# Two feed-forward networks with seven block products in place of eight, in a one-core decoder layer

## The chip, the core and the metric

The kernel runs on one core of a Trainium2 chip. The core has five engines that run side by side, each in the order of its own queue: TensorE (PE in the profile; its weight loads have a row of their own, PEld), VectorE (DVE), ScalarE (ACT), GpSimd (POOL) and SyncE (SP), which here only issues DMA transfers. TensorE writes its sums to PSUM, eight banks of 128 partitions x 512 floats; the other operands lie in SBUF, 128 partitions wide, and device memory is reached by DMA. An engine waits for another on a semaphore.

The metric is the device time of one execution in microseconds. Lower is better.

## The reference

One layer of a hybrid decoder, for 1024 prompt tokens and 8 decoding sequences of one token, 1032 tokens together, with 1024 features each:

```python
def swiglu_half(x, g, w_gate, w_up, w_down):
    u = rmsnorm(x, g)
    return x + 0.5 * ((jax.nn.silu(u @ w_gate) * (u @ w_up)) @ w_down)

def hybrid_layer(...):
    h = swiglu_half(x, ffn1_norm, ...)          # 1024 -> 2816 -> 1024
    u = rmsnorm(h, mix_norm); z = u @ w_in      # latent attention, retention, two gates
    ...
    h = h + merged @ w_out
    h = swiglu_half(h, ffn2_norm, ...)
    gate = sigmoid(rmsnorm(h, ple_norm) @ w_ple_gate)
    return h + gate * (p_emb @ w_ple_proj)      # and a last rmsnorm
```

The change touches the two `swiglu_half` calls and what lies directly ahead of and behind them. Each is three products: 1032 x 1024 by 1024 x 2816 (gate and up) and 1032 x 2816 by 2816 x 1024 (down).

## The kernel before

Activations lie with the features on the partitions: a tile of 128 features by tokens. The tokens are cut into three chunks of 344 (`CHUNKS`). Every large product works on float32 values that are split in two: a high part in the format that TensorE takes at full rate (fp32r), made by a cast on ScalarE (L93), and the rest, made by a subtraction on VectorE (L94). `mm3` (L127 to L130) then multiplies high by high, high by low and low by high into one PSUM bank: three matmuls where plain arithmetic has one. A weight tile, 128 outputs by 1024 inputs, comes through `Ring.load` (L101): a DMA on SyncE's queue, then the split.

An FFN (`ffn`, L221) runs over the 22 blocks of 128 hidden features in groups of three (the last has four). For each block and chunk it makes the gate product and the up product, eight blocks of the inner dimension each (L230, L232), multiplies both by the reciprocal root `r` of the norm, applies Silu, multiplies, and splits the result into `mid` (L235 to L241). At the end of a group the down product adds its part to the residual `h` in SBUF (L274).

The norm is spread out. `norm_steps` (L183) multiplies the residual by the gain and splits it (L199 on ScalarE, L200 on VectorE), sums the squares (L148, then L149 on GpSimd), and `rstd` (L162) adds over the partitions with small matmuls (L169), takes the reciprocal root by three Newton steps on VectorE, and spreads it with matmuls (L177). The factor `r` is applied after the products, so that these need not wait for it. The steps of the next stage's norm are run one at a time between the products of the last group: `next(steps)` at L276 and in `wout` (ahead of FFN 2), with what remains kept in `pend` and drawn by `tick`. The residual stays in SBUF through an FFN; after FFN 1 a copy goes to device memory (`hs_d`, L331, on GpSimd's queue) and is read back at the merge (L1002).

After FFN 1 come the value tiles of the retention (`value_tile`, L314), 128 tokens by 256 columns over eight blocks of the inner dimension, whose evacuation needs `RT`, the factor `r` with tokens on partitions. After FFN 2 come the gate products of the per-layer embedding (`ple_gate`, L1034), over columns 0 to 400, 400 to 776 and 776 to 1032.

The order on each engine isn't that of the text. A planner takes the text's order as priority and fills an engine's free time with later instructions that it reckons to be ready; so in the first microseconds ScalarE works on `u` (L199) ahead of the weight cast (L93) that stands before it in the text. PSUM banks are taken in turn: 0 to 3 for products (`bank`), 4 to 7 for the norm and the retention (`cbank`).

## Time and profile before

| what | value |
|---|---|
| time of three runs, median (lowest to highest) | 2559.01 us (2556.11 to 2561.74) |
| profiled execution, its span | 2553.2 us (the page gives no other time of it; 5.8 us below the median of the runs) |
| TensorE busy | 2519.5 us, 99%, 16612 matmuls |
| VectorE, ScalarE, GpSimd busy | 49%, 26%, 8% |
| FFN 1, first FFN matmul to last | 7.6 to 778.8 us |
| FFN 2, first FFN matmul to last | 1665.6 to 2418.6 us |
| mean granted clock of TensorE | 0.996 of full speed |
| DMA | 171.08 MB, 67 GB/s on average |

The span runs from the first instruction to the last; what lies around it (the start and the end of the program) is not in the profile. Busy time of TensorE counts a matmul from its start to its modelled end, and these overlap, so the number to read is the pitch from one start to the next. In a group's row the parts are: source line, engine, operation, outputs and inputs with their shapes, the count, then busy microseconds and the mean nanoseconds of one, then the idle time ahead of it and what ended it. A row of a time stretch gives its length, then busy time and count for TensorE, its weight loads, VectorE, ScalarE and GpSimd, then the granted clock, the DMA share and GB/s. A row in order of time begins with start and duration in microseconds.

### The profile page before, as it was taken

To read this page: it belongs to the slowest core of one execution; us is meant where nothing else is said; L and a number is where in the kernel's file an instruction comes from. 1 tells how busy PE (TensorE), PEld (TensorE's weight loads), DVE (VectorE), ACT (ScalarE), POOL (GpSimd) and SP (SyncE) were. 2 spreads that over 40 slices of the span, in tenths; PEclk is the share of its full clock that TensorE was granted. 3 is DMA by queue.
4 is the path that set the end of the run, shared out by engine and by line. 5 is a ranking of instruction groups with operands and counts; after the bars stand their busy time and mean duration, and the time that the engine had idled before them with its cause. 6 is when DMAs were issued, how large, how long until landed. Compare 5 with 4: busy or idle time off the path is not lost.

```text
span 2553.2 us, 40552 instructions
## 1 busy us (share of the span) xinstructions
PE 2519.5 (99%) x16612; PEld 2433.6 (95%) x16612; DVE 1251.2 (49%) x2744; ACT 655.8 (26%) x1302; POOL 209.6 (8%) x247
## 2 busy tenths in 40 slices
...
GB/s 151 42 59 51 41 59 42 50 42 34 58 71 117 62 77 58 98 77 64 54 78 129 121 107 217 51 58 42 50 42 44 53 53 34 58 42 50 40 36 67
DMA packets 82507, 171.08 MB, mean 67 GB/s; under 512 B 9401, under 2 KB 51586, under 8 KB 82322
## 3 DMA queue, kind: packets, MB, share of 16 engines
...
q8 instruction: 130, 2.13, 0.3%
q14 instruction: 55, 0.45, 0.1%
...
## 4 chain that ended last, share of the span: by engine, by line
PE 94%; DVE 3%; DMA 1%; ACT 1%; issue 1%; POOL 0%; SPq 0%; POOLq 0%; DVEq 0%; ACTq 0%
PE ps L128 27%; PE ps L129 27%; PE ps L130 27%; PE ps L732 2%; PE ps L768 1%; PE ps L757 1%; PE ps L177 1%; PE ps L323 1%; PE ps L321 1%; PE ps L322 1%; DVE u L200 1%; PE ps L169 1%; DMA raw<-in_wout_dram 0%; PE ps L906 0%; PE ps L880 0%
## 5 line engine op out<-in xcount | busy, mean ns | idle before, releaser
L128 PE MATMUL ps<-u,w 128*128 128x344 f32 (+2 forms) x3072 | 990.6, 323 | 7.6 <-ACT w L93 7.6
L129 PE MATMUL ps<-u,w 128*128 128x344 f32 (+2 forms) x3072 | 987.0, 321 | 3.5 <-DVE u L200 3.5
L130 PE MATMUL ps<-u,w 128*128 128x344 f32 (+2 forms) x3072 | 982.8, 320 | 0.1
L128 PEld LDWEIGHTS ps<-u,w 128*128 128x128 f32 x3072 | 578.4, 188 | 9.6 <-ACT w L93 7.6
L129 PEld LDWEIGHTS ps<-u,w 128*128 128x128 f32 x3072 | 577.2, 188 | 6.4 <-DVE u L200 5.5
L130 PEld LDWEIGHTS ps<-u,w 128*128 128x128 f32 x3072 | 577.9, 188 | 1.1 <-DVE w L94 0.5
L93 ACT CAST w<-raw 128x1024 fp32r<-128x1024 f32 (+1 forms) x198 | 203.4, 1042 | 776.7 <-PE ps L130 757.0
L130 PE MATMUL ps<-mid,w 128*128 128x344 f32 x1248 | 399.7, 320 | 0.1
L129 PE MATMUL ps<-mid,w 128*128 128x344 f32 x1248 | 399.7, 320 | 0.0
L128 PE MATMUL ps<-mid,w 128*128 128x344 f32 x1248 | 399.6, 320 | 0.0
L274 DVE SCALAR_TENSOR_TENSOR h<-ps,h 128x344 f32<-128x344 f32 x336 | 172.0, 515 | 242.0 <-PE ps L130 239.8
L94 DVE TENSOR_TENSOR w<-raw,w 128x1024 fp32r<-128x1024 f32 (+1 forms) x198 | 239.1, 1219 | 63.5 <-ACT w L93 63.0
L130 PEld LDWEIGHTS ps<-mid,w 128*128 128x128 f32 x1248 | 235.4, 189 | 0.4 <-DVE w L94 0.4
L128 PEld LDWEIGHTS ps<-mid,w 128*128 128x128 f32 x1248 | 235.2, 188 | 0.0
L129 PEld LDWEIGHTS ps<-mid,w 128*128 128x128 f32 x1248 | 235.0, 188 | 0.0
L238 DVE TENSOR_TENSOR m<-ps,r 128x344 f32<-128x344 f32 x132 | 68.1, 516 | 336.4 <-PE ps L130 336.4
L149 POOL TENSOR_TENSOR acc<-acc,sq 128x344 f32<-128x344 f32 x83 | 84.1, 1013 | 1677.9 <-ACT sq L148 1676.6
L93 ACT CAST mid<-m 128x344 fp32r<-128x344 f32 x156 | 74.9, 480 | 353.3 <-DVE m L239 316.6
L235 DVE TENSOR_TENSOR sg<-ps,r 128x344 f32<-128x344 f32 x132 | 68.0, 515 | 167.5 <-PE ps L130 166.0
L236 ACT ACTIVATE sg<-sg 128x344 f32<-128x344 f32 x132 | 64.6, 489 | 227.8 <-DVE sg L235 227.8
L94 DVE TENSOR_TENSOR mid<-m,mid 128x344 fp32r<-128x344 f32 x156 | 80.9, 519 | 48.0 <-ACT mid L93 46.9
L200 DVE SCALAR_TENSOR_TENSOR u<-h,gains,u 128x344 fp32r<-128x344 f32 x96 | 65.1, 686 | 30.7 <-ACT u L199 30.6
(247 smaller groups left out, 2321.4 us busy)
## 6 DMA issues: line engine op xcount, KB each, us to landing
ct<-in_cache_dram SPq DMA_DIRECT2D x128, 128.0 KB, 2.1
...
hs_d<-h POOLq DMA_DIRECT2D x3, 1376.0 KB, 6.1
```

The source lines that it names most:

```text
L93: act.copy(dst_hi, src)
L94: dve.tensor_tensor(dst_lo, src, dst_hi.bitcast(F32), op=ALU.subtract)
L128: pe.matmul(ps, w[:, 0, ws], x[:, 0, xs], start=start, stop=False)
L129: pe.matmul(ps, w[:, 0, ws], x[:, 1, xs], start=False, stop=False)
L130: pe.matmul(ps, w[:, 1, ws], x[:, 0, xs], start=False, stop=stop)
L149: pool.tensor_tensor(acc, acc, sq[:, :n], op=ALU.add)
L200: dve.scalar_tensor_tensor(u[k][:, 1, xs], h[k][:, xs], gain(gi, k), u[k][:, 0, xs].bitcast(F32), op0=ALU.mult, op1=ALU.subtract)
L235: dve.tensor_tensor(s[:, :n], pg[:, :n], r[:, xs], op=ALU.mult)
L236: act.activation(s[:, :n], s[:, :n], AF.Silu)
L238: dve.tensor_tensor(m[:, :n], pu[:, :n], r[:, xs], op=ALU.mult)
L274: dve.scalar_tensor_tensor(hv, ps[:, :n], 0.5, hv, op0=ALU.mult, op1=ALU.add)
L732: pe.matmul(ps[:, :w], qc[hd][:, i * P:(i + 1) * P], kc[hd][:, j:j + w], start=True, stop=not diag)
```

## The change

Both FFNs compute each product as a two by two block product with seven multiplications in place of eight (the Winograd form of Strassen's method). The output tiles are taken in pairs, the inner dimension is halved, and the tokens are cut into two halves (`TPS`) of two quarters of 258 (`HC`). The multiplications need sums and differences of the blocks on both sides, and the results need sums.

- On the weight side `Stream` loads four 128 x 512 pieces (four DMAs on SyncE's queue), makes four sums on GpSimd and splits seven operands. `take` keeps five operands ahead.
- On the token side `build` makes seven operands for each half: four differences on VectorE and seven splits. For gate and up they are built once an FFN, over eight blocks of the inner dimension. For down they are built four times, once a group (`GROUPS`: blocks 0 to 5, 6 to 11, 12 to 17, 18 to 21), in place, while the last unit of the group before still runs (`paced_build`, one step after each product, after a lag).
- `unit` does the seven multiplications of one pair of output tiles, for one or both halves. Three PSUM accumulators x, y, z take them; x is read out after products 0, 2 and 4 while later products go on adding to it, z after 4 and 6. The four output blocks are sums of these readings, made by the evacuation functions (`gate`, `up`, `add`). x takes banks 0 to 3, y 4 and 5, z 6 and 7; a unit of both halves uses two of each.
- The norm is applied ahead of the products: `start` sums the squares of a half, takes `r`, scales the residual, then builds. It runs entirely ahead of the first unit for the first half, and in steps between the products of the first two units for the second. The first gate unit and the first up unit are done for one half at a time, so the first two weight units are loaded and split twice.
- The gated values go to device memory (`mid1_d`, `mid2_d`) and are read back for the down products. The residual is read again at the down products, and the FFN's result is stored (`hs_d`, `h3_d`). The merge stores its result to `h2_d` for FFN 2.
- The norms behind each FFN (before the retention and before the per-layer embedding), and the one ahead of FFN 2, no longer run between products: the residual is read back and `norm_steps` runs chunk by chunk. `ring` is now two rings, the first closed before FFN 2.
- `w_down` is laid out in column tiles, as gate and up are. `ident` is loaded first. The scratch for DMAs that GpSimd issues is set to 4096 bytes (`dynamic_dma_scratch_size`).

The core of the diff; the removed `ffn`, `first_weights` and `to_mix` are in the listing above, and comments that it takes out are left out:

```diff
+HC = T // 4
+TPS = (0, 1)
...
+    def cols(tp, lr):
+        return slice((2 * tp + lr) * HC, (2 * tp + lr + 1) * HC)
+    class Stream:
+        def __init__(self, wp, rawp, units, ahead):
+            self.wp, self.rawp, self.ahead = wp, rawp, ahead
+            self.ready, self.made = [], self.make(units)
+        def load(self, name, m1, m2, k0, kh):
+            n = kh * P
+            out = []
+            for m in (m1, m2):
+                for k in (k0, k0 + kh):
+                    t = self.rawp.tile([P, 512], F32, tag="q", name="wq")
+                    sp.dma_start(t[:, :n], a[name][m][:, k * P:k * P + n])
+                    out.append(t[:, :n])
+            return out
+        def split(self, src):
+            n = src.shape[-1]
+            w = self.wp.tile([P, 2, 512], F32R, tag="w", name="w")
+            split(w[:, 0, :n], w[:, 1, :n], src)
+            return w
+        def make(self, units):
+            nxt = self.load(*units[0])
+            for i in range(len(units)):
+                a11, a12, a21, a22 = nxt
+                n = a11.shape[-1]
+                s1 = self.rawp.tile([P, 512], F32, tag="q", name="ws")[:, :n]
+                pool.tensor_tensor(s1, a21, a22, op=ALU.add)
+                if i + 1 < len(units):
+                    nxt = self.load(*units[i + 1])
+                yield self.split(a11)
+                pool.tensor_tensor(a21, a11, a21, op=ALU.subtract)
+                yield self.split(s1)
+                pool.tensor_tensor(s1, s1, a11, op=ALU.subtract)
+                yield self.split(s1)
+                yield self.split(a12)
+                pool.tensor_tensor(a12, a12, s1, op=ALU.subtract)
+                yield self.split(a21)
+                yield self.split(a22)
+                yield self.split(a12)
+        def take(self):
+            while len(self.ready) <= self.ahead:
+                w = next(self.made, None)
+                if w is None:
+                    break
+                self.ready.append(w)
+            return self.ready.pop(0)
+    xbank, ybank, zbank = rotation(0, 4), rotation(4, 2), rotation(6, 2)
+    def unit(stream, bs, kh, tps, evac, tick=lambda: None):
+        x, y, z = ({tp: b() for tp in tps} for b in (xbank, ybank, zbank))
+        for q in range(7):
+            w = stream.take()
+            for tp in tps:
+                ps = (x, z, x, y, x, x, z)[q][tp][:, :HC]
+                b = bs[q][tp]
+                for j in range(kh):
+                    js = slice(j * P, (j + 1) * P)
+                    pe.matmul(ps, w[:, 0, js], b[:, 0, j], start=q in (0, 1, 3) and j == 0, stop=False,
+                              skip_group_check=True)
+                    pe.matmul(ps, w[:, 0, js], b[:, 1, j], start=False, stop=False, skip_group_check=True)
+                    pe.matmul(ps, w[:, 1, js], b[:, 0, j], start=False, stop=j == kh - 1, skip_group_check=True)
+                evac(q, tp, x[tp][:, :HC], y[tp][:, :HC], z[tp][:, :HC])
+                tick()
+    def build(q4, bs, kh, tps):
+        for q in range(7):
+            for tp in tps:
+                b11, b12, b21, b22 = q4[tp]
+                if q == 1:
+                    dve.tensor_tensor(b11, b12, b11, op=ALU.subtract)
+                elif q == 2:
+                    dve.tensor_tensor(b12, b22, b12, op=ALU.subtract)
+                    dve.tensor_tensor(b11, b22, b11, op=ALU.subtract)
+                elif q == 5:
+                    dve.tensor_tensor(b21, b21, b11, op=ALU.subtract)
+                b = bs[q][tp]
+                split(b[:, 0, :kh], b[:, 1, :kh], (b11, b11, b11, b21, b12, b21, b22)[q])
+                yield
+    def ffn(pre, gi, src, dst, mid_d):
+        GROUPS = [(0, 3), (6, 3), (12, 3), (18, 2)]
+        st = ExitStack()
+        wp = st.enter_context(pools(pre + "w", 7))
+        rawp = st.enter_context(pools(pre + "q", 9))
+        e = st.enter_context(pools(pre + "e", 18))
+        first = [(pre + n, 0, 1, 0, 4) for n in ("gate", "up")]
+        units = first + [(pre + n, 2 * i, 2 * i + 1, 0, 4) for i in range(NF // 2) for n in ("gate", "up")]
+        units += [(pre + "down", 2 * o, 2 * o + 1, k0, kh) for k0, kh in GROUPS for o in range(KT // 2)]
+        stream = Stream(wp, rawp, units, 5)
...
+        b_st = ExitStack()
+        bp = b_st.enter_context(pools(pre + "b"))
+        tiles = operands(bp, 4)
+        bs = [[tiles[q, tp] for tp in TPS] for q in range(7)]
+        with pools(pre + "x", side="right") as xp:
+            ht = xp.tile([P, KT, T], F32, name="ht")
+            sq = [xp.tile([P, HC], F32, name=f"sq{i}", tag=f"sq{i}") for i in range(3)]
+            r = xp.tile([P, T], F32, name="r")
+            for tp in TPS:
+                ts = slice(2 * tp * HC, 2 * tp * HC + 2 * HC)
+                for k in (0, 4):
+                    sp.dma_start(ht[:, k:k + 4, ts], src[:, k:k + 4, ts])
+            def start(tp):
+                ts = slice(2 * tp * HC, 2 * tp * HC + 2 * HC)
+                acc = sq[2]
+                for lr in range(2):
+                    xs = cols(tp, lr)
+                    for k in range(KT):
+                        to = acc if k == 0 else sq[k % 2]
+                        act.activation(to, ht[:, k, xs], AF.Square)
+                        if k:
+                            dve.tensor_tensor(acc, acc, to, op=ALU.add)
+                    yield
+                    for _ in rstd([acc], HC, D, r[:, xs]):
+                        yield
+                for k in range(KT):
+                    dve.scalar_tensor_tensor(ht[:, k, ts], ht[:, k, ts], gain(gi, k), r[:, ts],
+                                             op0=ALU.mult, op1=ALU.mult)
+                    if k % 4 == 3:
+                        yield
+                q4 = {tp: [ht[:, 4 * i:4 * i + 4, cols(tp, lr)] for i in range(2) for lr in range(2)]}
+                yield from build(q4, bs, 4, (tp,))
+            for _ in start(0):
+                pass
+            later = start(1)
+            gated = {}
...
+            def gate(q, tp, x, y, z):
+                if q in (0, 2, 4):
+                    t = kept[tp, q] = tile_e()
+                    act.copy(t, x)
+                if q == 3:
+                    t, s, o = kept[tp, 0], y, 0
+                elif q == 4:
+                    t, s, o = kept[tp, 4], z, 3
+                elif q == 6:
+                    t, s, o = kept[tp, 2], z, 1
+                elif q == 5:
+                    t = gated[tp, 2] = tile_e()
+                    act.activation(t, x, AF.Silu)
+                    return
+                else:
+                    return
+                dve.tensor_tensor(t, t, s, op=ALU.add)
+                act.activation(t, t, AF.Silu)
+                gated[tp, o] = t
+            def up(f):
+                def evac(q, tp, x, y, z):
...
+                    if s is None:
+                        dve.tensor_tensor(t, x, gated[tp, o], op=ALU.mult)
+                    else:
+                        dve.tensor_tensor(t, t, s, op=ALU.add)
+                        dve.tensor_tensor(t, t, gated[tp, o], op=ALU.mult)
+                    sp.dma_start(mid_d[f + o // 2, :, cols(tp, o % 2)], t)
+                return evac
+            for tp in TPS:
+                for _ in later if tp else ():
+                    pass
+                unit(stream, bs, 4, (tp,), gate, step)
+                unit(stream, bs, 4, (tp,), up(0), step)
+        e2_st = ExitStack()
+        qp = e2_st.enter_context(pools(pre + "m", 8, side="right"))
+        def fetch(g):
+            k0, kh = GROUPS[g]
+            got = {}
+            for tp in TPS:
+                got[tp] = []
+                for i in range(2):
+                    for lr in range(2):
+                        t = qp.tile([P, 3, HC], F32, tag="m", name="m")[:, :kh]
+                        sp.dma_start(t, mid_d[k0 + i * kh:k0 + i * kh + kh, :, cols(tp, lr)]
+                                     .rearrange("k p t -> p k t"))
+                        got[tp].append(t)
+            return got
+        def paced_build(lag, q4, bs, kh):
+            for _ in range(lag):
+                yield
+            yield from build(q4, bs, kh, TPS)
+        for i in range(1, NF // 2):
+            if i == NF // 2 - 1:
+                q4 = fetch(0)
+            unit(stream, bs, 4, TPS, gate)
+            if i < NF // 2 - 1:
+                unit(stream, bs, 4, TPS, up(2 * i))
+            else:
+                b_st.close()
+                b_st = ExitStack()
+                bp = b_st.enter_context(pools(pre + "c"))
+                tiles = operands(bp, 3)
+                old, bs = bs, [[tiles[q, tp] for tp in TPS] for q in range(7)]
+                todo = paced_build(6, q4, bs, 3)
+                unit(stream, old, 4, TPS, up(2 * i), lambda: next(todo, None))
+                for _ in todo:
+                    pass
+        hp = e2_st.enter_context(pools(pre + "h", side="right"))
+        ht = hp.tile([P, KT, T], F32, name="ht2")
+        for o in range(0, KT, 2):
+            sp.dma_start(ht[:, o:o + 2], src[:, o:o + 2])
+        def add(o, last):
+            def evac(q, tp, x, y, z):
+                if q in (0, 2, 4):
+                    t = tile_e()
+                    act.activation(t, x, AF.Copy, scale=0.5)
+                    hv = ht[:, o + (q == 4), cols(tp, int(q > 0))]
+                    pool.tensor_tensor(hv, hv, t, op=ALU.add)
+                if q in (3, 4, 5, 6):
+                    s, i, lr = {3: (y, 0, 0), 4: (z, 1, 1), 5: (x, 1, 0), 6: (z, 0, 1)}[q]
+                    hv = ht[:, o + i, cols(tp, lr)]
+                    dve.scalar_tensor_tensor(hv, s, 0.5, hv, op0=ALU.mult, op1=ALU.add)
+                if last and q == 6:
+                    ts = slice(2 * tp * HC, 2 * tp * HC + 2 * HC)
+                    sp.dma_start(dst[:, o:o + 2, ts], ht[:, o:o + 2, ts])
+            return evac
+        for g, (k0, kh) in enumerate(GROUPS):
+            end = g + 1 == len(GROUPS)
+            if not end:
+                q4 = fetch(g + 1)
+            for o in range(0, KT, 2):
+                todo = iter(())
+                if not end and o == KT - 2:
+                    todo = paced_build(1, q4, bs, GROUPS[g + 1][1])
+                unit(stream, bs, kh, TPS, add(o, end), lambda: next(todo, None))
+                for _ in todo:
+                    pass
+        e2_st.close()
+        b_st.close()
+        st.close()
+    ffn("f1", 0, a["xT"], hs_d, mid1_d)
...
+    def read_h(ht, src):
+        for c0, n in CHUNKS:
+            for k in (0, 4):
+                sp.dma_start(ht[:, k:k + 4, c0:c0 + n], src[:, k:k + 4, c0:c0 + n])
...
+        read_h(ht, hs_d)
+        wv0 = [ring.load("rv", i) for i in range(2)]
+        for c in range(NCH):
+            for _ in norm_steps(tmp, h, c, 1, u, r):
+                pass
...
+            sp.dma_start(h2_d[:, :, c0:c0 + n], ht[:, :, c0:c0 + n])
...
+    ffn("f2", 2, h2_d, h3_d, mid2_d)
...
+    read_h(ht, h3_d)
+    plw = [ring.load("plg", o) for o in range(2)]
+    u, r = new_u(up)
+    for c in range(NCH):
+        for _ in norm_steps(tmp, h, c, 3, u, r):
+            pass
```

151 lines of the change are left out of this document (48 added, 103 removed).

## The prediction, on record before the changed kernel was run

> **What bounds the kernel now.** I read the page first, then the chain of waits, then the matmuls in order of time, and last the groups of instructions by shape on the engines that the change loads.
>
> ```profile
> span 2553.2 us, 40552 instructions
> PE 2519.5 (99%) x16612; PEld 2433.6 (95%) x16612; DVE 1251.2 (49%) x2744; ACT 655.8 (26%) x1302; POOL 209.6 (8%) x247
> ...
> PE 94%; DVE 3%; DMA 1%; ACT 1%; issue 1%; POOL 0%; SPq 0%; POOLq 0%; DVEq 0%; ACTq 0%
> ```
>
> TensorE is the path: 94% of the chain, and no other engine is half busy. So a matmul left out is worth its pitch (start to start) as long as TensorE never waits. The pitches and the borders of the FFNs come from the time stretches (the parenthesis after PE is the count of matmuls begun) and from the matmuls in order of time.
>
> ```profile
> 7.60:65.00 57.40, 53.49 (x302) 50.56 (x303) 43.94 (x83) 33.37 (x65) 21.66 (x20) 0.94 0.39 139
> 65.00:770.00 705.00, 704.54 (x4467) 704.29 (x4466) 291.74 (x506) 138.08 (x222) 16.77 (x18) 1.00 0.15 50
> 300.00:400.00 100.00, 100.00 (x635) 100.00 (x635) 38.81 (x66) 16.65 (x26) 0.00 (x0) 1.00 0.13 46
> ...
> 778.65 0.32 PE L130 MATMUL ps<-mid,w 128*128 128x344 f32 x1
> 778.81 0.28 PE L321 MATMUL ps<-w,u 128*128 128x256 f32 x1
> 781.54 0.28 PE L323 MATMUL ps<-w,u 128*128 128x256 f32 x1
> ...
> 1630.00:1668.00 38.00, 34.29 (x212) 33.37 (x211) 30.40 (x63) 21.16 (x45) 18.46 (x19) 0.96 0.00 1
> 1665.58 0.32 PE L128 MATMUL ps<-u,w 128*128 128x344 f32 x1
> ...
> 2418.44 0.32 PE L130 MATMUL ps<-mid,w 128*128 128x344 f32 x1
> 2418.60 0.35 PE L128 MATMUL ps<-u,w 128*128 128x400 f32 x1
> ```
>
> 344 columns: 100/635 = 157.5 ns. 256 columns: 23 pitches from 778.81 to 781.54, 118.7 ns. The slope is 0.44 ns a column, so 258 columns cost 119.5 ns (estimate). FFN 1 ends at 778.8. FFN 2 runs from 1665.6 to 2418.6, 753.0 us. The other 1021.4 us stay, less some 4 us of waits for the norm ahead of 1665, which move (38.0 - 212 x 0.1575 = 4.6 between 1630 and 1668). One FFN holds 22 column tiles x 2 weights x 3 chunks x 8 k x 3 terms = 3168 matmuls, and 22 x 8 x 3 x 3 = 1584 for the down product: 4752, or 748.4 us. So 30.4 us of FFN 1 are not products (start-up, most of it before 65) and 4.6 us of FFN 2.
>
> **The products.** Afterwards an FFN has 22 units x 7 products x 2 token halves x 4 k x 3 terms = 3696 matmuls, and 4 x 7 x 2 x 11 x 3 = 1848 for down: 5544 of 258 columns, 662.5 us. Both save 85.9 us, together 172. Columns fall by 1/8; time falls by 11.5%, since shorter matmuls carry a larger fixed part.
>
> **What one vector instruction costs.** These rows price the operands that must now be made.
>
> ```profile
> 24.17 0.52 DVE L235 TENSOR_TENSOR sg<-ps,r 128x344 f32<-128x344 f32 x1 [0.97 <-ACT r L180]
> 24.61 0.51 DVE L238 TENSOR_TENSOR m<-ps,r 128x344 f32<-128x344 f32 x1
> ...
> 782.54 1.21 DVE L94 TENSOR_TENSOR w<-raw,w 128x1024 fp32r<-128x1024 f32 x1
> 783.68 0.56 DVE L200 SCALAR_TENSOR_TENSOR u<-h,gains,u 128x344 fp32r<-128x344 f32 x1
> ...
> L93 ACT CAST w<-raw 128x1024 fp32r<-128x1024 f32 x195 | 201.7, 1049 | 772.1 <-PE ps L130 752.4 <-DMA raw<-in_batt_dram 12.9 <-DMA raw<-in_wout_dram 3.3
> L199 ACT ACTIVATE u<-h,gains 128x344 fp32r<-128x344 f32 x96 | 55.1, 579 | 63.5 <-DVE h L274 42.7 <-DVE h L980 15.8 <-DMA h<-in_xT_dram 4.4
> L148 ACT ACTIVATE sq<-h 128x344 f32<-128x344 f32 x80 | 38.1, 477 | 1.1 <-POOL acc L149 1.1
> ...
> L200 DVE SCALAR_TENSOR_TENSOR u<-h,gains,u x96: 562/576/1344, 5.8 to 2423.5; 128x344 fp32r<-128x344 f32 x96
> L149 POOL TENSOR_TENSOR acc<-acc,sq x83: 912/932/1782, 7.1 to 2419.4; 128x344 f32<-128x344 f32 x83
> L444 POOL TENSOR_TENSOR qd<-qT,qdec x8: 1281/1292/2293, 817.7 to 1023.4; 128x512 f32<-128x512 f32 x8
> ```
>
> VectorE's pitch is 0.44 us at 344 columns and 1.14 at 1024, so 0.35 at 258, 0.48 at 384, 0.61 at 512, 0.88 at 774, 1.15 at 1032. GpSimd takes 0.93 at 344 and 1.29 at 512 (about 1.0 at 384, 0.7 at 258). The two collide: L200 with both operands in SBUF goes from 0.58 to 1.34, L149 from 0.91 to 1.78, and where they run together they alternate:
>
> ```profile
> 29.80 4.67 POOL L149 TENSOR_TENSOR acc<-acc,sq 128x344 f32<-128x344 f32 x4 [0.45 <-ACT sq L148]
> 33.63 2.42 DVE L200 SCALAR_TENSOR_TENSOR u<-h,gains,u 128x344 fp32r<-128x344 f32 x2
> ```
>
> One GpSimd and one VectorE instruction take 1.17 to 1.21 us together, against 0.93 + 0.44 one after the other: some 80% of GpSimd's time is added to VectorE's. The Trainium skill says the same more strictly (SBUF — State Buffer, "Who interferes with whom"): a VectorE instruction with two SBUF inputs and a GpSimd instruction that reads SBUF exclude each other for their whole length. By that rule 100% would be added, which makes the sum below about 15 us longer; the rows show less, and I go by them. Each weight unit puts four GpSimd sums and seven VectorE splits on that port, where the FFN loops had no GpSimd work.
>
> In the steady part this is hidden: a unit of 168 matmuls lasts 20.1 us, and VectorE needs 7 x 0.61 + 14 x 0.35 = 9.2 and GpSimd 5.2. Not so at four places.
>
> **Start of an FFN: 54 us.** Nothing is multiplied until the half's norm is known and b0 built. Then VectorE is the limit.
>
> ```profile
> 0.00:7.60 7.60, 0.00 (x0) 0.00 (x0) 1.25 (x4) 3.85 (x8) 0.69 (x5) 1.00 0.70 225
> 0.00:20.00 20.00, 10.94 (x50) 9.36 (x51) 11.30 (x16) 13.11 (x24) 8.69 (x11) 1.00 0.91 318
> ...
> 18.69 0.83 PE L169 MATMUL ps<-ones,acc 128*128 128x1 f32 x6 [0.31 <-POOL acc L149]
> ...
> 22.76 0.90 PE L177 MATMUL ps<-ident,nz 128*128 128x128 f32 x6
> ```
>
> The last column is GB/s: 1.7 MB are in by 7.6 and 6.4 MB by 20, so the half's two 1.05 MB pieces, now the first in the queue, land at about 7 and 10. Eight squares and sums take 4 us for each of two quarters, and the chain from the sum to the spread reciprocal root is 4.1 us: r at about 22.5. From there VectorE owes 16 scalings x 0.62, two builds of 11 x 1.15, 21 splits x 0.61, 14 sums x 0.35, 20 evacuations x 0.35 and 3.6 of Newton steps: 63.7 us, with 80% of 12 GpSimd sums x 1.29, 12 us, on top. It is done at 98; the last evacuations and fillings of earlier gaps take off 4. TensorE has four half units of 84 matmuls in that time, 40.1 us. Lost 54 (41 without collisions, 61 with the builds' ScalarE casts of 1.05 us exposed). In FFN 2 the residual goes out and comes back first; its last chunk's write ends late, but the first half needs only the earlier chunks: 55 (45 to 65).
>
> **Changes of the contraction group: 28 us an FFN.** Around each, 14 operands are built from 22 instructions, and all of VectorE's other work stands in the same queue: 22 x 0.88 + 10 splits x 0.48 + 8 evacuations x 0.35 = 27 us from 2 us into the last unit, and 80% of the part of GpSimd's 16 us (weights and residual sums of two units) that meets it, 7: 36 and a last product of 1.1, while the two units are 30.1 us of products. TensorE loses 6.5, and 1.5 more since its clock falls back:
>
> ```profile
> PE ps L177 <- DVE nz L137: 3.4, 2, 2.2
> ...
> 1662.34 0.49 PE L128 MATMUL ps<-mid,w 128*128 128x344 f32 x1
> 1662.63 0.49 PE L129 MATMUL ps<-mid,w 128*128 128x344 f32 x1
> ```
>
> Here, 2 us after a 2.2 us wait, the pitch is 0.29 in place of 0.16. So 8 for each of two changes. The short group's builds are 22 x 0.62 = 13.6 in place of 19.4: 5, between hidden and as long. From up to down the builds start 8 us into the unit, when b2 has been read, and with the unit's 7 us of other work and 4 of collisions end at 39 against 35.1 of products: 5, with the clock 7. Bounds: 4 if nothing collides; 50 if the z banks (two, each needed again in the next unit) are freed only after every build ahead of their evacuation in the queue.
>
> **Norm after each FFN: 21 and 23 us.** Before, it ran under the last products. Now they are in line behind the last product:
>
> ```profile
> out_y_dram<-h SPq DMA_DIRECT2D x4, 400.0 KB, 3.6
> ```
>
> The store of 0.5 MB lands at about +3 and the read of chunk 0's second half at +6.5. ScalarE's 8 casts and 8 squares of a chunk are 8.4 us by the rows above: chunk 0 is ready at +12, chunk 1 at +20.5, chunk 2 at +29. After FFN 1 four value tiles fit into this; a fifth needs a bank, so an evacuation, so r of chunk 1, 6.5 us after the chunk, +27. TensorE is busy from +29, with 11 us of products before, some of them late or at the low clock: 21 (13, where only chunk 0 is waited for, to 28). After FFN 2 the first gate product is 400 columns wide and needs chunk 1: 23 (17 to 32).
>
> **Small waits in the down units: 14 us.** Product 4 is cast, summed by GpSimd, then VectorE adds z, and only then may product 6 go on in that bank: 2 to 3 us against 3.2 of other products, 2.2 in the short group. About 0.4 us in 32 units (0 to 0.9).
>
> **Queues and the detour.**
>
> ```profile
> L103 SPq DMA_DIRECT2D raw<-in_f1gate_dram x22: 327/328/2642, 1.7 to 639.8; - x22
> ...
> hs_d<-h POOLq DMA_DIRECT2D x3, 1376.0 KB, 6.1
> sg<-ga_d SPq DMA_DIRECT2D x24, 172.0 KB, 4.0
> kt<-in_kpeT_dram,idk POOLq DMA_INDIRECT x32, 2.6
> ```
>
> SyncE now issues 8 weight loads and 8 stores of gated values in a gate and an up unit: 16 x 0.33 = 5.3 of 40 us. A store waits there for VectorE and holds the loads behind it, but those are due a unit (20 us) later. DMA is 13% busy in the FFN loops (row 300 to 400), so the gated values, read back a unit ahead, cost nothing; exposed, it would be a read of 4 to 6 us a group. The norms leave GpSimd's queue at the end of an FFN, as do the stores to hs_d, with nothing critical behind them. The smaller scratch for DMAs issued by GpSimd meets the gathers of the attention first; issued ahead, 0, and up to 10 if each waits for its 2.6 us.
>
> **The sum.** 1021.4 - 4 + 2 x 662.5 = 2342.4 without losses; with 54 + 55 + 2 x 28 + 21 + 23 + 14 = 223 it is 2565 against 2553.2. The runs' median lies 5.8 above the span (2559.0), so 2571. Break-even is a loss of 211. The saving is eaten by serial starts and joins.
>
> **Rivals.** First, faster: the joins stay fed. What decides is the collision at the group changes; the forecast has 7 us for each of eight; below 5.5 the sum turns. For it: VectorE alone would fit, 29 of 30 us, and the planner does let matmuls pass one that waits, as here the second term of pT:
>
> ```profile
> 2424.22 0.43 PE L128 MATMUL ps<-pT,w 128*128 128x400 f32 x1
> 2424.49 0.33 PE L128 MATMUL ps<-u,w 128*128 128x376 f32 x1
> ...
> 2425.51 0.35 PE L129 MATMUL ps<-pT,w 128*128 128x400 f32 x1
> ```
>
>  Against it: the rows of the collision. Starts 48 + 49, groups 20, norms 40, small waits 5: 162, so 2504 and 2510 with the 5.8. Second, much slower: the queue order frees the z banks late. For it: VectorE runs in order, and the order was planned without collisions. Groups 88, starts 118, norms 48, small waits 24: 278, so 2626. Against it: four x banks let TensorE go on. Third: a matmul's fixed part is larger than I read it, so that fewer columns save nothing. The 118.7 ns at 256 columns speaks against it. At 0.9 of the 344 pitch, 141.8 ns, the products would be 786 us and the time 2818. The Trainium skill has that slope (TensorE: Matmul & The Clock Gate, "Back-to-back issue gap"): sustained 81 ns at 128 columns and 131 at 512, so 98 at 258 against 109 at 344, an estimate. The trace does not agree: 157.5 at 344.
>
> **How the numbers follow.** Forecast (2540 to 2600) 0.43, fed joins 0.33, late banks 0.22, fixed part 0.02. Four fifths lie between 2505 and 2640; the forecast's own range is 2540 to 2600. 0.2% is 5 us, about what a measurement here can tell from no change. Below 2554: the fed joins and 0.05 of the forecast, 0.38. Within 2554 to 2564: 0.11. Above: 0.51.
>
> **What would show it.** Right: 11,088 matmuls of 258 columns at 119 to 120 ns inside a unit; first product near 29 us and full units from about 94; VectorE near 9 tenths busy and GpSimd's mean above 1.5 us at the starts; TensorE gaps behind VectorE at the group changes. Wrong: a pitch above 121 ns; gaps below 5.5 us at each change (faster) or above 12 (much slower); gaps in the middle of every unit, which I expect nowhere.

## The result

| | before | after |
|---|---|---|
| time, median of 4 runs each, us | 2557.9 | 2653.6 (2651.9 to 2656.8) |
| ratio, 95% interval | | 1.037 [1.036, 1.039] |
| profiled span, us | 2553.2 | 2651.6 |
| mean granted TensorE clock | 0.996 | 0.965 |

The change makes the kernel 96 us slower. The forecast was 2571, its range ended at 2640: the direction was right, the size was not. The page of the changed kernel begins:

```profile
span 2651.6 us, 47356 instructions
PE 2440.1 (92%) x18208; PEld 2323.9 (88%) x18208; DVE 1593.3 (60%) x3285; ACT 1005.0 (38%) x2207; POOL 758.3 (29%) x716
```

TensorE is still the busiest engine, but its share falls from 99% to 92%. Where the rest went, the time stretches show. Each is cut at a first or last product; the columns are the stretch and its length, busy time (instructions begun) of TensorE, weight loads, VectorE, ScalarE and GpSimd, then granted clock, DMA share and GB/s:

```profile
0.00:29.70 29.70, 7.01 (x30) 6.70 (x30) 16.46 (x51) 14.77 (x34) 2.77 (x6) 1.00 0.60 216
29.70:113.70 84.00, 56.78 (x355) 51.22 (x356) 73.83 (x111) 41.50 (x73) 29.93 (x19) 0.94 0.18 59
113.70:496.70 383.00, 383.00 (x3194) 383.00 (x3193) 182.78 (x324) 148.96 (x326) 106.84 (x78) 1.00 0.29 88
496.70:780.30 283.60, 258.50 (x2019) 250.03 (x2017) 207.37 (x343) 125.91 (x272) 155.90 (x158) 0.98 0.33 103
780.30:829.20 48.90, 28.23 (x154) 24.68 (x152) 36.01 (x64) 30.30 (x64) 24.21 (x24) 0.72 0.50 178
1697.90:1732.10 34.20, 7.18 (x32) 6.64 (x31) 15.86 (x53) 12.58 (x30) 0.00 (x0) 0.56 0.49 165
1732.10:1810.60 78.50, 58.58 (x355) 55.53 (x356) 73.31 (x104) 38.66 (x68) 23.45 (x16) 0.78 0.16 49
2193.80:2479.00 285.20, 260.70 (x2019) 252.72 (x2017) 208.00 (x343) 125.78 (x272) 156.65 (x158) 0.96 0.33 102
2479.00:2530.00 51.00, 26.45 (x123) 22.60 (x121) 37.69 (x70) 32.37 (x64) 21.14 (x20) 0.70 0.47 163
```

The third row is the steady part of FFN 1: 3194 products in 383.0 us, 0.120 us each, TensorE busy throughout. Nearly all that is lost lies in the other rows: the two starts, the down parts with their changes of group, and the norms behind the FFNs. One column misleads at the start: the record of the granted clock begins at 53 us, and up to there the rows show 1.00, though the products between 29 and 53 us start 0.21 us apart, as they do at half clock. In the forecast's terms (us lost against 0.120 us a product; norms against 886.8 - 4 and 134.6 before):

| term | forecast | measured | how |
|---|---|---|---|
| pitch | 0 | 5.5 | 11,088 x 0.5 ns |
| start, FFN 1 and 2 | 54 + 55 | 73.3 + 72.3 | 336th product at 113.5, and 112.5 after the merge's last, less 335 x 0.12 |
| steady part | 0 | 0.1 + 0.4 | 3193 pitches each |
| down part: group changes and small waits | 35 + 35 | 41.5 + 43.2 | last 2015 pitches of each FFN |
| norms | 21 + 23 | 34.9 + 38.1 | 917.7 from the last product of FFN 1 to the merge's last; 172.7 from that of FFN 2 to the end |
| sum | 223 | 309 | 2342.4 + 309 = 2651 |

### The profile page after: what moved, and what is told of

It is laid out like the page before. It is cut to its first block, busy times and chain, and to the rows that moved or that the text cites. A ratio compares the mean times of both kernels' runs of the same rounds, so it can differ in the third digit from the quotient of the medians.

```text
span 2651.6 us, 47356 instructions
## 1 busy us (share of the span) xinstructions
PE 2440.1 (92%) x18208; PEld 2323.9 (88%) x18208; DVE 1593.3 (60%) x3285; ACT 1005.0 (38%) x2207; POOL 758.3 (29%) x716
## 5 line engine op out<-in xcount | busy, mean ns | idle before, releaser
L300 PE MATMUL ps<-b,w 128*128 128x258 f32 x3696 | 1066.4, 290 | 76.5 <-ACT b L100 25.0
L302 PE MATMUL ps<-b,w 128*128 128x258 f32 x3696 | 1061.0, 288 | 17.2 <-DVE b L101 17.2
L303 PE MATMUL ps<-b,w 128*128 128x258 f32 x3696 | 1051.1, 287 | 6.4 <-DVE w L101 6.4
L300 PEld LDWEIGHTS ps<-b,w 128*128 128x128 f32 x3696 | 714.0, 193 | 94.4 <-ACT b L100 28.7
L302 PEld LDWEIGHTS ps<-b,w 128*128 128x128 f32 x3696 | 715.6, 194 | 21.0 <-DVE b L101 20.7
L303 PEld LDWEIGHTS ps<-b,w 128*128 128x128 f32 x3696 | 710.9, 193 | 9.2 <-DVE w L101 9.2
L101 DVE TENSOR_TENSOR w<-wq,w 128x512 fp32r<-128x512 f32 (+2 forms) x400 | 275.0, 693 | 178.1 <-ACT w L100 169.5
L100 ACT CAST w<-wq 128x512 fp32r<-128x512 f32 (+2 forms) x400 | 223.1, 567 | 256.6 <-PE ps L303 140.5
L136 PE MATMUL ps<-u,w 128*128 128x344 f32 (+4 forms) x960 | 310.9, 324 | 4.4 <-DVE u L207 4.4
L135 PE MATMUL ps<-u,w 128*128 128x344 f32 (+4 forms) x960 | 312.8, 326 | 1.7 <-DVE s L1261 1.7
L137 PE MATMUL ps<-u,w 128*128 128x344 f32 (+4 forms) x960 | 309.3, 322 | 0.0
L101 DVE TENSOR_TENSOR w<-ws,w 128x512 fp32r<-128x512 f32 (+2 forms) x160 | 119.2, 745 | 226.8 <-ACT w L100 226.6
L486 POOL TENSOR_TENSOR ht<-ht,e 128x258 f32<-128x258 f32 x192 | 185.0, 974 | 164.8 <-ACT e L484 150.7
L136 PEld LDWEIGHTS ps<-u,w 128*128 128x128 f32 (+1 forms) x960 | 180.6, 188 | 8.0 <-DVE u L207 7.1
L135 PEld LDWEIGHTS ps<-u,w 128*128 128x128 f32 (+1 forms) x960 | 181.4, 189 | 4.0 <-DVE s L1261 2.0
L137 PEld LDWEIGHTS ps<-u,w 128*128 128x128 f32 (+1 forms) x960 | 181.1, 189 | 0.6
L100 ACT CAST w<-raw 128x1024 fp32r<-128x1024 f32 (+1 forms) x65 | 67.1, 1044 | 203.6 <-PE ps L137 172.8
L490 DVE SCALAR_TENSOR_TENSOR ht<-ps,ht 128x258 f32<-128x258 f32 x256 | 101.5, 419 | 59.1 <-POOL ht L486 47.1
L276 POOL TENSOR_TENSOR wq<-wq,ws 128x512 f32<-128x512 f32 (+2 forms) x80 | 97.5, 1219 | 118.5 <-DVE w L101 85.2
```

The lines of the kernel that those rows point to most:

```text
L100: act.copy(dst_hi, src)
L101: dve.tensor_tensor(dst_lo, src, dst_hi.bitcast(F32), op=ALU.subtract)
L135: pe.matmul(ps, w[:, 0, ws], x[:, 0, xs], start=start, stop=False)
L136: pe.matmul(ps, w[:, 0, ws], x[:, 1, xs], start=False, stop=False)
L137: pe.matmul(ps, w[:, 1, ws], x[:, 0, xs], start=False, stop=stop)
L276: pool.tensor_tensor(a12, a12, s1, op=ALU.subtract)
```

## The experiments

Each kernel is timed beside the kernel before (medians 2553.6 to 2557.9; 2553.6 beside kernels 12 to 15, so a few microseconds between kernels of different rounds show nothing by themselves). Kernels 2 and 6 leave sums or differences out and so multiply other operands; they bound what those cost. "Start" is the 336th product, the last of the first gate and up units (in FFN 2 counted from the merge's last), "down" the loss of the last 2015 pitches, "mid" and "end" as in the norms' row above; all from the profiled execution. The expectations call a change of group a join. The order of instructions is planned anew in every kernel, so a stretch that an edit doesn't touch can move too: by up to 4 us as a rule, by 8 once (start 2 of kernel 14).

| kernel | built on | us | start 1 | start 2 | down 1 | down 2 | mid | end |
|---|---|---|---|---|---|---|---|---|
| after | | 2653.6 | 113.5 | 112.5 | 41.5 | 43.2 | 917.7 | 172.7 |
| 1 weight sums on VectorE | after | 2607.9 | 107.7 | 102.5 | 30.0 | 30.1 | 915.5 | 170.3 |
| 2 weight sums out | after | 2588.7 | 103.5 | 101.6 | 23.9 | 23.9 | 914.8 | 170.1 |
| 3 norm sums on VectorE | after | 2640.1 | 114.8 | 111.7 | 41.6 | 43.1 | 912.8 | 165.1 |
| 4 residual adds on VectorE | after | 2662.0 | 115.4 | 111.8 | 47.3 | 46.4 | 916.2 | 172.6 |
| 5 both halves together | 1 | 2600.0 | 99.8 | 100.4 | 30.6 | 30.0 | 917.8 | 171.7 |
| 6 differences out | 1 | 2557.1 | 97.5 | 91.6 | 14.6 | 16.1 | 918.1 | 172.4 |
| 7 extra matmuls | 1 | 2619.4 | 107.2 | 105.9 | 29.0 | 28.9 | 923.0 | 171.7 |
| 8 squares summed by TensorE | 1 | 2648.8 | 128.9 | 121.9 | 30.5 | 28.9 | 914.8 | 171.2 |
| 9 norm behind the products | 5 | 2570.8 | 85.6 | 84.6 | 29.2 | 29.0 | 920.5 | 171.5 |
| 10 and norm sums on VectorE | 9 | 2558.3 | 85.9 | 83.5 | 29.0 | 30.1 | 911.5 | 166.0 |
| 11 and residual kept in SBUF | 10 | 2536.2 | 85.2 | 79.2 | 30.5 | 30.2 | 902.5 | 157.7 |
| 12 first weights early | 1 | 2607.0 | 107.3 | 103.9 | 31.2 | 28.9 | 911.7 | 170.8 |
| 13 weight sums back on GpSimd | 11 | 2568.0 | 92.9 | 81.1 | 43.7 | 42.7 | 898.9 | 157.7 |
| 14 transposes in pairs | 11 | 2526.5 | 85.1 | 70.8 | 30.5 | 31.6 | 898.2 | 158.1 |
| 15 edits 12 and 14 | 11 | 2524.5 | 84.4 | 70.8 | 30.1 | 29.9 | 898.0 | 157.3 |
| 16 shorter Newton chain | 15 | 2524.6 | 88.3 | 72.5 | 29.0 | 30.0 | 898.3 | 156.6 |

**1 and 2: the weight sums.** Three theories stood against each other: collisions of GpSimd with VectorE, more VectorE work than counted, and TensorE's half clock.

```diff
-                pool.tensor_tensor(s1, a21, a22, op=ALU.add)
+                dve.tensor_tensor(s1, a21, a22, op=ALU.add)
...
```

> The four sums of each weight unit move from GpSimd to VectorE; nothing else is edited. Collision theory (the unpriced time is GpSimd sums that stop VectorE, and with it ScalarE, for their whole length of 1.3 to 1.9 us): the 336th product of FFN 1 is done near 100 us in place of 113.5, the same in FFN 2, and each of the eight joins of the down part loses 2 us less; 2653 - 13 - 13 - 16 = 2611. Work theory (VectorE has simply more to do at the starts than I counted; a collision adds the 80% of my sum): a sum costs 0.61 us in place of 1.03, so 5 us a start and 1 us a join less, 2635. Clock theory (the unpriced time is TensorE at half clock after its waits): nothing but what shorter waits bring, 2640 to 2653.

> The four sums of each weight unit are left out, so raw pieces are multiplied in place of the sums and the output is not the reference's; the splits, the matmuls and the DMAs all stay. It bounds what the weight sums cost wherever they run. Collision theory: 20 us less at each start, 4 us less at each join, 2653 - 40 - 32 = 2581. Work theory: 12 us a start and 2 a join, 2653 - 24 - 16 = 2613. Clock theory: 2630 or above.

Edit 1 takes off 45.7 us, edit 2 takes off 64.9. The total of edit 1 is the collision theory's (2611), its places are not: the starts give 6 and 10 in place of 13 each, the down parts 11.5 and 13.1 in place of 8. For the starts the work theory was nearer. What a collision looks like, in the order of time in the changed kernel (two answers, VectorE and GpSimd; start, length, instruction):

```profile
54.78 0.15 DVE L144 SCALAR_TENSOR_TENSOR nz<-nt,nz 128x3 f32<-128x3 f32 x1
54.85 0.42 DVE L364 TENSOR_TENSOR sq<-sq,sq 128x258 f32<-128x258 f32 x1
55.19 1.25 DVE L142 TENSOR_TENSOR nt<-nv,nz 128x3 f32<-128x3 f32 x1
...
54.94 1.48 POOL L273 TENSOR_TENSOR ws<-ws,wq 128x512 f32<-128x512 f32 x1 [3.21 <-DVE nz L144]
```

A three-element step of the Newton iteration, 0.15 us when alone, lasts 1.25 us here and ends with GpSimd's sum (56.44 and 56.42). And without any sums, the start of FFN 1 stays long:

```profile
29.50:103.70 74.20, 59.04 (x362) 54.95 (x362) 63.01 (x112) 39.18 (x70) 0.00 (x0) 0.93 0.22 68
```

VectorE is busy 63.0 us here against 73.8 with the sums (the second row of the stretches above): the collisions cost 10.8 us at this start, where the forecast had 12. But in both, VectorE is also idle for 10 to 11 us, which the forecast hadn't.

**3 and 4: GpSimd's two other jobs.**

```diff
-            pool.tensor_tensor(acc, acc, sq[:, :n], op=ALU.add)
+            dve.tensor_tensor(acc, acc, sq[:, :n], op=ALU.add)
```

> In the two norms behind the FFNs the running sum of squares moves from GpSimd to VectorE; the FFNs are not edited. After: from the last product of FFN 1 to the last product of the merge 917.7 us, from the last product of FFN 2 to the end 172.6. Collision theory: a step of the norm is paced by GpSimd's 1.155 us and falls to ScalarE's 1.01 or below, and the small Newton steps are no longer stretched: 9 us less in each, 2635. Serial theory (the round trip through device memory, the chain and the order of the matmuls set it): 24 steps by 0.15, of which only the first chunk's eight are in front of TensorE, 1 to 3 us each, 2648.

```diff
-                    act.activation(t, x, AF.Copy, scale=0.5)
-                    pool.tensor_tensor(hv, hv, t, op=ALU.add)
+                    dve.scalar_tensor_tensor(hv, x, 0.5, hv, op0=ALU.mult, op1=ALU.add)
```

> In the down part the readings of x after products 0, 2 and 4 go to the residual straight from PSUM on VectorE (0.35 us each); the ScalarE cast and the GpSimd addition (0.97 us mean) go. Only the down part of both FFNs should move; it loses 41.5 and 43.2 us after. Collision theory: 12 additions around each join cost VectorE 0.35 in place of 80% of 0.7 to 1.0, 3 to 5 us less a join, 2653 - 8 x 4 = 2621. Work theory: VectorE's queue stays as long (4.2 us in place of 6.7), 1 to 2 us a join, 2641. Late banks: the x banks now come free behind the builds in VectorE's queue, 2 us more a join, 2669.

Edit 3 gives 4.9 and 7.6 us, between the two theories. Edit 4 is slower by 8: not the collision, but the late banks, at half of what was expected of them. TensorE's waits around the change from the first to the second group in FFN 1 (us, times, longest), in the changed kernel and in edit 4:

```profile
PE ps L300 <- ACT e L484: 2.7, 3, 1.3
PE ps L302 <- DVE b L101: 0.6, 1, 0.6
```

```profile
PE ps L300 <- DVE ht L488: 3.4, 2, 3.2
PE ps L300 <- DVE ht L484: 3.3, 2, 2.1
```

In edit 4 TensorE waits for banks that VectorE reads out behind its builds. ScalarE's casts had kept x out of that queue; taking GpSimd's collisions away didn't pay for it.

**5 and 6: VectorE's own work.**

```diff
-            for tp in TPS:
-                unit(stream, bs, 4, (tp,), gate, step)
-                unit(stream, bs, 4, (tp,), up(0), step)
+            unit(stream, bs, 4, TPS, gate, step)
...
+            unit(stream, bs, 4, TPS, up(0))
```

> Built on the kernel with the weight sums on VectorE (2607.9; 336th product at 107.7 us in FFN 1 and 102.5 after the merge's last product in FFN 2). Both token halves are made ready side by side, and the first gate and up units run over both, so their two weight units are loaded, summed and split once. Work theory (VectorE has no free time between the norm and the 336th product): 14 splits and 8 sums of 0.61 us fewer, 13 us, of which the filling of the next units takes some back: 10 us a start, 2588, although the first product comes some 12 us later. Serial theory (TensorE's wait for its first product sets the stage): those 12 us are lost at both starts, 2632.

```diff
-                    dve.tensor_tensor(b11, b12, b11, op=ALU.subtract)
...
-                    dve.tensor_tensor(b21, b21, b11, op=ALU.subtract)
```

> Built on the kernel with the weight sums on VectorE (2607.9; joins and down part 30 us an FFN). The four differences of the token side's operands are left out of each build, so raw blocks are multiplied and the output is not the reference's; splits, matmuls and DMAs all stay. Work theory: VectorE owes 8 x 1.15 us less at each start and 7 us less at each full join: 9 us a start and 3 a join, 2608 - 18 - 24 = 2566. Serial or clock theory: the stages keep most of their length, 2590 to 2608.

Edit 5 gives 8 and 2 us at the starts, less than the 13 us of VectorE's work it removes, and the first product of FFN 1 is hardly later (29.5 against 29.0). Edit 6 agrees with the work theory, and more: 10.2 and 10.9 at the starts for 9.2 us of work, 15.4 and 14.0 in the down parts where 12 was expected. The stretch of two units around the change from the first to the second group, of edit 1, then of edit 6:

```profile
568.57:587.60 19.03, 15.52 (x128) 15.11 (x127) 17.48 (x22) 11.96 (x22) 8.10 (x8) 1.00 0.08 22
587.60:605.12 17.52, 17.19 (x127) 16.78 (x127) 17.02 (x29) 8.06 (x17) 4.40 (x6) 0.90 0.69 206
```

```profile
551.99:568.66 16.67, 15.39 (x128) 15.19 (x127) 15.04 (x22) 13.94 (x25) 5.60 (x6) 1.00 0.27 72
568.66:585.24 16.58, 15.79 (x128) 15.28 (x127) 15.51 (x28) 6.80 (x16) 5.05 (x6) 1.00 0.65 193
```

126 products are 15.1 us. In the first unit of edit 1 VectorE is busy 17.5 of 19.0 us and TensorE 15.5; with less work for VectorE the unit is 2.4 us shorter. So the sums of work at starts and group changes had the right limit.

**7 and 8: work for TensorE that misses.**

```diff
             act.activation(u[k][:, 0, xs], h[k][:, xs], AF.Copy, scale=gain(gi, k))
+            pe.matmul(fill[:, :n], ones, u[k][:, 0, xs].bitcast(F32), start=True, stop=True)
```

> Built on the kernel with the weight sums on VectorE (2607.9). In the norms behind the FFNs one extra matmul of 344 columns (its result is not read) follows each of the 24 casts, so that TensorE has work while it waits for the norm. Clock theory: the granted clock stays at 1.0 between 763 and 815 us and after the last product of FFN 2, and TensorE's products there run at full pitch: 4 us less after FFN 1, 5 after FFN 2, 2599. Serial theory: the norm sets these stretches, the clock only fills waits: 2608, or up to 5 more, where an extra matmul stands ahead of a product.

```diff
-                        if k:
-                            dve.tensor_tensor(acc, acc, to, op=ALU.add)
...
-                    for _ in rstd([acc], HC, D, r[:, xs]):
+                    for _ in rstd(sq, HC, D, r[:, xs]):
```

> Built on the kernel with the weight sums on VectorE (2607.9). At the start of an FFN the 28 additions of squares on VectorE go; TensorE sums the eight squared blocks in its one-column matmuls (24 a quarter in place of 3). Work theory: 28 x 0.35 = 9.8 us less for VectorE, 9 us a start, 2590. Serial theory: only the first quarter's additions are ahead of the first product: 1 to 2 us a start, 2605.

Ten microseconds behind FFN 1 in edit 7, then in edit 1 (its last product is at 761.2 and 762.8):

```profile
770.00:780.00 10.00, 8.01 (x23) 4.48 (x24) 10.00 (x10) 9.27 (x22) 8.42 (x8) 0.82 1.06 387
```

```profile
770.00:780.00 10.00, 7.85 (x30) 6.67 (x31) 10.00 (x11) 9.24 (x20) 6.97 (x7) 0.51 1.06 385
```

Edit 7 raises the clock from 0.51 to 0.82 there and lengthens the stretch behind FFN 1 by 7.5. So the half clock isn't shown to cost anything in the norms; as the extra matmuls also stand in the queue and move the value products (the 24 behind FFN 1 keep TensorE busy for 21.5 us), what a full clock alone would bring stays open. Edit 8 is 41 us slower than edit 1, where both theories had it faster:

```profile
11.67 10.38 PE L176 MATMUL ps<-ones,sq 128*128 128x1 f32 x48
21.91 1.42 PE L184 MATMUL ps<-ident,nz 128*128 128x128 f32 x6
23.19 7.39 PE L176 MATMUL ps<-ones,sq 128*128 128x1 f32 x34
32.80 1.44 PE L184 MATMUL ps<-ident,nz 128*128 128x128 f32 x6 [2.22 <-DVE nz L144]
```

A record of a one-column matmul takes 0.216 us (10.38 / 48), and each of these matmuls leaves two records, 48 for the 24 of a quarter of the tokens: so the sums of a quarter cost TensorE 10.4 us, and those of two quarters stand ahead of the second root, which comes at 32.8 where edit 1 has it at 23.2. Neither theory had this, and both starts lose 20.

**9: the norm behind the products**, as it was before the change; the other parts of the change stay.

```diff
-                    dve.scalar_tensor_tensor(ht[:, k, ts], ht[:, k, ts], gain(gi, k), r[:, ts],
-                                             op0=ALU.mult, op1=ALU.mult)
+                    if tp:
+                        act.activation(ht[:, k, ts], ht[:, k, ts], AF.Copy, scale=gain(gi, k))
+                    else:
+                        dve.tensor_scalar(ht[:, k, ts], ht[:, k, ts], gain(gi, k), None, op0=ALU.mult)
...
                 dve.tensor_tensor(t, t, s, op=ALU.add)
+                dve.tensor_tensor(t, t, rs, op=ALU.mult)
                 act.activation(t, t, AF.Silu)
+                dve.tensor_tensor(t, t, rs, op=ALU.mult)
```

> Built on the kernel with the weight sums on VectorE and both halves together (2600.0; 336th product at 99.8 in FFN 1, 100.4 after the merge's last product in FFN 2). The norm of both FFNs goes behind the gate and up products, as it was in the kernel before the change: operands are built from gain times residual, the reciprocal root multiplies the gate's four outputs (twice, 16 more VectorE instructions of 0.35 us in a gate unit). Work theory, with the start's order as its second half: VectorE was idle for 18 of the first 26 us because everything waited for the norm, and owed 10 us of scalings behind it; the 336th product comes near 75, and 25 us earlier in FFN 2 too: 2550. Serial theory (the pieces' arrival, ScalarE's casts and squares then set the start): 10 us a start, 2580. If the 16 extra instructions show in the steady part: 22 x 2 x 1 us worse than either.

14.2 and 15.8 us a start, 29 in all: between the theories. VectorE is now at work before the root is known, and so is ScalarE, which is full there (same columns as above):

```profile
10.00:20.00 10.00, 1.44 (x6) 1.35 (x6) 10.00 (x25) 9.75 (x25) 0.00 (x0) 1.00 1.01 377
20.00:26.00 6.00, 2.37 (x9) 2.07 (x9) 6.00 (x13) 6.00 (x13) 0.00 (x0) 1.00 0.02 5
26.00:86.00 60.00, 51.76 (x373) 49.51 (x373) 56.00 (x129) 30.65 (x56) 0.00 (x0) 0.94 0.18 55
```

The 16 extra instructions in a gate unit cost nothing in the steady part (0.1 us lost).

**10 and 11: the norms behind the FFNs.** Edit 10 is edit 3 again. Edit 11:

```diff
-        ht = hp.tile([P, KT, T], F32, name="ht2")
...
-        ht, h = new_h(hp)
-        read_h(ht, hs_d)
+        h = [ht[:, k, :] for k in range(KT)]
```

> The kernel with the norm behind the products, and the running sums of squares of the two norms behind the FFNs moved from GpSimd to VectorE, as in the earlier run of this edit alone, which gave 11.5 us. If the terms add up: 11 to 12 us below the kernel with the norm behind the products. If what was gained was the collision with the weights' or the tables' GpSimd work: under 5.

> The kernel before this one in the list, and the residual stays in SBUF between an FFN and the norm behind it: the read back from device memory (4.2 MB, behind the store of the last pieces) goes; the store for the merge stays, that of FFN 2 goes too. The gated values of the first down group are fetched into the tile of the residual to make room. Serial theory: the first value product came 9 us after the last product, 6 of them the round trip, and the later chunks' reads ran 4 us behind: 6 to 8 us less in each of the two places, 14 in all. If the norm's steps on ScalarE and VectorE set these stretches whatever the read does: 3 us each.

12.5 and 22.1 us. The norm sums add up with the other edits (edit 3 alone gave 13.5 by the medians; the 11.5 of the expectation is the figure of no run); keeping the residual gives 9.0 and 8.3 at the two places, a little above the serial theory, and this version is faster than before: 0.991 [0.989, 0.993].

**12 to 16: what is left of the starts and norms.**

```diff
                     sp.dma_start(ht[:, k:k + 4, ts], src[:, k:k + 4, ts])
+                if tp == 0:
+                    stream.prime()
```

> Built on the kernel with the weight sums on VectorE (2607.9; 336th product at 107.7 us and 102.5 after the merge). The first unit's four weight pieces (1 MB) are asked for ahead of the second half of the residual, not behind it. Late weights theory (my sum let the first seven splits fill VectorE's gaps before the norm is known, but the pieces land near 20 us): 7 splits and 4 sums of 0.61 us move into idle time, 5 to 7 us a start, 2596. Order theory (VectorE's early gaps are too short, or the second half of the residual, 3 us later, is then what is late): within 3 us of 2608.

```diff
-                dve.tensor_tensor(s1, a21, a22, op=ALU.add)
+                pool.tensor_tensor(s1, a21, a22, op=ALU.add)
...
```

> The fastest kernel so far (2536.2: sums and norm sums on VectorE, both halves together, norm behind the products, residual kept in SBUF), with the four sums of each weight unit put back on GpSimd. Undone in the changed kernel this edit gave 45 us: 25 at the joins, 16 at the starts, 4 at the norms. If collisions cost the same wherever VectorE is the bound: 2536 + 40 = 2576. If they mattered only beside the scalings and norm sums that are gone or moved: the joins alone, 2561. If it is the queue order of that one kernel: under 10.

```diff
-            for t0 in range(0, NT, 4):
+            for t0 in range(0, NT, 2):
...
```

> The fastest kernel so far (2536.2), with the reciprocal roots of the retention's value tiles transposed for two token tiles at a time in place of four, so that tiles 0 and 1 can be read out when the first chunk's norm is known. Between 761.0 and 766.1 us TensorE stands still there behind the second chunk's root. Order theory: the stop goes or shrinks, 3 to 5 us less after FFN 1, 2532. Serial theory (VectorE's and ScalarE's steps for the next chunk set the stretch, only the place of the stop moves): within 2 us.

> The fastest kernel so far (2536.2) with both edits: the first weight unit asked for ahead of the second half of the residual, and the transposes in pairs. Late weights theory and order theory together: 2536 - 10 - 4 = 2522. If both fail: 2536, or a few us more, since both halves are wanted early in this kernel and the second comes 3 us later.

```diff
-        for _ in range(3):
+        for _ in range(2):
             dve.tensor_tensor(t, v, y, op=ALU.mult)
```

> The fastest kernel so far (2524.5: both edits of the run before), with two steps of the Newton iteration for each reciprocal root in place of three, everywhere (one step, so some accuracy of the roots, is left out). Between 759.4 and 764.7 us each of the chain's eleven small instructions on VectorE stands behind a 0.5 us instruction of the next chunk, and TensorE stands still for 5 us. Order theory (the queue stretches the chain): three instructions fewer take 1.7 us off each such chain that is in front of TensorE, one or two behind FFN 1, one or two behind FFN 2 and the last norm: 4 us less in all, 2520. Theory that the next chunk's steps set the end whatever the chain does: within 1 us of 2524.

Edit 12 changes nothing (2607.0 against 2607.9; the first product even comes at 36.0 in place of 29.0): late weights fall as a cause. In edit 15 the first product even comes at 14.6 us in place of 25.2, and the 336th at 84.4 in place of 85.2: the first product doesn't set the start. Edit 13 costs 31.8, of which 25.7 in the down parts: there a collision costs the same in another order; at the starts 7.7 and 1.9, where the first two weight units are now made once and not twice. Edit 14 gives 9.7 us, but not as expected: the stop is still there (4.78 us of waiting in edits 11, 14 and 15 alike), mid falls by 4.3 elsewhere, and 8.4 come off FFN 2's start, which the edit doesn't touch: most of the gain comes with the new order of instructions and is luck. Edit 16 shortens the stop as the order theory says, and mid doesn't move. Edit 15, then edit 16:

```profile
764.88 1.58 PE L184 MATMUL ps<-ident,nz 128*128 128x128 f32 x6 [4.78 <-DVE nz L144]
```

```profile
765.40 1.58 PE L184 MATMUL ps<-ident,nz 128*128 128x128 f32 x6 [3.23 <-DVE nz L144]
```

4.78 becomes 3.23, mid is 898.0 and 898.3, as the second theory has it; that the next chunk's steps are what is late then is argued, not shown. Edits 14, 15 and 16 lie within 2 us and can't be told apart by their times. Of edit 15, 2524.5 us, 0.989 [0.987, 0.990] of before: it is 29 us under the kernel before in the same rounds, and 129 under the change as it was made.

## Why the prediction was wrong

**Right.** The pitch: 0.120 us for 258 columns against 0.1195; the third rival (a larger fixed part) is out. The steady units lose nothing, and DMA hides the detour there. VectorE is the limit at the starts and group changes (edits 5, 6). Serial starts and joins eat the saving. The clock at the group changes was sized well: products at half clock cost 5.1 and 7.7 us in the two down parts, 1.3 and 1.9 a change, where the forecast had 1.5.

**The starts: 109 forecast, 146 measured.** The step that failed is the credit: "the last evacuations and fillings of earlier gaps take off 4". VectorE's work was sized well in all, in part by luck. From the first scaling to the 336th product of FFN 1 it is busy 77.5 us, the sum had 63.7 + 12; but it makes 32 splits of weights in this time, not 21, and adds 7 squares, not 14. And it isn't continuously busy: it stands still for 10 of these 88 us, most of it behind ScalarE's casts (the first scaling, and its two largest waits up to 104 us):

```profile
25.83 2.76 DVE L369 SCALAR_TENSOR_TENSOR ht<-ht,gains,r 128x516 f32<-128x516 f32 x4 [0.41 <-ACT r L187]
...
DVE b L101 <- ACT b L100: 4.1, 2, 3.3
DVE w L101 <- ACT w L100: 3.2, 2, 1.7
```

In edit 2 it stands still as long, but more for TensorE than for ScalarE, so what recurs is the waiting in order and not one wait. So +10 in place of -4, the root 3.3 us later than worked out, 2 more of work: that is the 19.3 missing in FFN 1. In FFN 2 17.3 are missing: the first scaling comes 30.3 us after the merge's last product, 7 later than worked out (ScalarE's squares wait for the residual that is read back, the first until 6.9 us and the fifth until 13.4), and VectorE stands still for 5 of the 82 us that follow. The collisions, 12 us in the sum and 10.8 here, agree by luck: GpSimd makes 19 sums in this stretch, not 12, and each adds 0.6 us to VectorE, not 1.0. By the Trainium skill (SBUF — State Buffer, "Who interferes with whom") the two exclude each other for their whole length; nineteen sums of 1.29 us would add 24.5 (an estimate), and the trace has less at this start; why isn't settled.

**The group changes: 70 forecast, 85 measured.** The small waits inside a unit, 14 us, hardly exist: units that stand beside no change lose 0.3 us or less. The changes themselves lose 85, not 56, and half of what is missing lies in one place. From up to down 13.9 and 15.1 us are lost in the two FFNs, where the sum had 7; each change between full groups loses 9.2 to 9.9, where it had 8, and that to the short group 8.2 and 8.7, where it had 5. The step that failed is "From up to down the builds start 8 us into the unit, when b2 has been read". The last up unit of FFN 1 and the first down unit, then what ScalarE and VectorE do around their border at 516.97 (start, length, instruction):

```profile
496.80:516.97 20.17, 20.17 (x170) 20.17 (x169) 9.80 (x20) 8.11 (x17) 4.05 (x4) 1.00 0.27 80
516.97:542.33 25.36, 17.95 (x129) 15.78 (x127) 22.79 (x30) 11.66 (x21) 17.92 (x6) 1.00 0.91 316
...
514.75 3.79 ACT L100 CAST b<-m 128x774 fp32r<-128x774 f32 x5
517.98 1.83 DVE L101 TENSOR_TENSOR b<-m,b 128x774 fp32r<-128x774 f32 x2
...
539.35 0.43 DVE L490 SCALAR_TENSOR_TENSOR ht<-ps,ht 128x258 f32<-128x258 f32 x1 [0.63 <-POOL ht L486]
```

The first cast of the builds comes 18 us into the up unit, not 8, behind casts of weights in ScalarE's queue. VectorE is busy for 9.8 of the unit's 20.2 us; then it builds all 14 operands in one block, 517.98 to 537.2, and only behind them reads an accumulator. Why the casts come so late stays open, and no run tried to start them earlier. The weight sums are not the cause: without them 10.4 us are lost there, with them on VectorE 12.1.

At the other changes the sum was nearer. In it the collision, "80% of the part of GpSimd's 16 us that meets it, 7", made all of the 6.5 us of loss at a change (its own terms, 36 + 1.1 - 30.1, give 7.0). Leaving out only the weight sums takes off 17.6 and 19.3 of the 41.5 and 43.2, 4.6 a change, and moving them to VectorE 11.5 and 13.1 (edits 1, 2, 13); the operands' differences are worth 15.4 and 14.0 (edit 6). What the rest of GpSimd's work costs there, the residual sums, is not known: edit 4, which moved them, brought another wait.

**The norms: 44 forecast, 73 measured.** The step that failed is "chunk 0 is ready at +12, chunk 1 at +20.5, chunk 2 at +29 ... TensorE is busy from +29". In it the chunks follow one another at ScalarE's 8.4 us. In the trace the first cast comes 8.3 us after the last product, behind three casts of weights, and the three roots reach ScalarE 26.5, 38.5 and 49.9 us after it, 12 us apart. The copy of a root (L187) stands in ScalarE's queue ahead of the next chunk's last casts, so ScalarE waits there for each chain over TensorE and VectorE, 4.1 and 4.4 us:

```profile
785.63 2.94 ACT L100 CAST w<-raw 128x1024 fp32r<-128x1024 f32 x3 [7.70 <-DMA hs_d<-ht]
...
806.64 0.45 ACT L187 COPY r<-ps 128x344 f32<-128x344 f32 x1 [4.11 <-PE ps L184]
...
818.67 0.45 ACT L187 COPY r<-ps 128x344 f32<-128x344 f32 x1 [4.38 <-PE ps L184]
```

Besides, GpSimd and VectorE are in each other's way:

```profile
790.42 13.86 POOL L156 TENSOR_TENSOR acc<-acc,sq 128x344 f32<-128x344 f32 x12 [11.77 <-issue]
...
790.12 9.80 DVE L207 SCALAR_TENSOR_TENSOR u<-h,gains,u 128x344 fp32r<-128x344 f32 x9
```

12 additions in 13.86 us, 1.155 a step, so 9.2 us a chunk in place of 8.4. TensorE then waits behind the second root, and its products between run at half clock; the waits between 780 and 830, and a stretch in which the clock is at half:

```profile
PE ps L545 <- ACT u L206: 8.7, 1, 8.7
PE ps L184 <- DVE nz L144: 6.3, 2, 5.3
...
789.11:797.80 8.69, 7.85 (x31) 6.67 (x32) 8.69 (x9) 7.95 (x18) 6.91 (x7) 0.53 1.06 384
```

It runs without stops only from 829, 49 us after the last product, not 29. The norm sums (edit 10) and the round trip (edit 11) together take off 18.0 us behind FFN 1 and 13.8 behind FFN 2; what is left, 19.7 and 23.1, is about what had been forecast with both in place.

**The rivals.** The fed joins are out with collisions in place; but with the sums moved, the norm behind and the round trip gone, the loss is small enough for the kernel to win. The late banks are in part what happened: that rival had 88 us at the changes, 85 were measured, and most of TensorE's waits in FFN 1's down part, 17.6 of 24.8 us, are for accumulators that are still to be read out (us, times, longest):

```profile
PE ps L300 <- ACT e L484: 10.1, 9, 2.7
PE ps L300 <- DVE ht L490: 7.5, 10, 2.1
```

From up to down VectorE reads y and z behind the last build, as the rival has it; the larger part is x, which ScalarE reads. Edit 4 shows what x costs behind VectorE's builds. The measured loss is above that rival's 278 because starts and norms went further than any case: their bounds (41 to 61 and 45 to 65; 13 to 28 and 17 to 32) all lay below what was measured, so the range was too narrow in these two terms.
